# ConvFFN of a hybrid decoder trunk: three products in PSUM banks of their own, block sums made by stores that add, weight sums on VectorE

## The chip, the cores and the metric

The kernel runs on one core of a Trainium2 chip. The metric is the device time of one execution in microseconds, as the median of several runs. Profiled executions are recorded by the hardware profiler; the engines are named as in its page: PE (TensorE matmul), PEld (TensorE weight load), DVE (VectorE), ACT (ScalarE), POOL (GpSimd), SP (the queue that issues most DMAs).

## What is computed

A two-layer decoder trunk on one sequence of 1024 tokens with 1024 features, in float32. Each layer mixes tokens (layer 0: gated linear attention, layer 1: sparse attention, both with memory attention) and then runs a ConvFFN. The change touches the ConvFFN only, which runs twice:

```python
def conv_ffn(h, w_up, conv_w, conv_b, w_down):
    T = h.shape[1]
    a, b = jnp.split(h @ w_up, 2, axis=-1)
    a_pad = jnp.pad(a, ((0, 0), (CONV_WIDTH - 1, 0), (0, 0)))
    a = sum(a_pad[:, j:j + T] * conv_w[j] for j in range(CONV_WIDTH)) + conv_b
    return (jax.nn.silu(a) * b) @ w_down

# in the layer loop
x = x + conv_ffn(rmsnorm(x, g_ffn[l]), w_up[l], conv_w[l], conv_b[l], w_down[l])
```

FFN_DIM is 2816, that is 22 tiles of 128.

## The kernel before

**Number format.** Every float32 operand is split into a rounded part and a remainder, both float32r. A product of two such operands takes three matmuls: high by high, high by low, low by high (lines 1058 to 1060 in the up-projection, 1412 to 1414 in the down-projection). ACT writes the high part (line 1022, tiles `Ah` and `A`), DVE subtracts it from the source for the low part (line 1023, tiles `Al` and `A`).

**The up-projection** works on 22 units (class `Up`), one for each 128 columns of `a` and of `b`. A unit is a 2 by 2 by 2 block product (two halves of the features, `a` and `b`, two halves of the tokens) that is made with seven half-size products instead of eight, the scheme of Strassen and Winograd. `B[1]` to `B[7]` are the seven right-hand operands, made once. The left-hand operands 3, 5, 6 and 7 are sums of the unit's four raw weight blocks; method `sums` makes them in place with four additions or subtractions of 128x512 (lines 1042 to 1045), on DVE for the first four units in order and on POOL for the other 18. Each product is 4 x 3 = 12 matmuls of 128x512.

The products of a unit go into PSUM like this. Products 1 and 2 build the first half of `a` in bank `fx`; product 1 alone is kept as `s1`. Product 6 opens bank `fy`, and DVE adds `s1` to it and keeps the sum as `q` (line 1092). Product 7 goes on adding into the same bank `fy`, and DVE keeps that with `s1` as `t` (line 1097). Product 4 adds into `fy` a third time (line 1106). Products 5 and 3 share bank `fw` in the same way (lines 1102 and 1112). There are eight banks, handed out in turn.

Each half then goes through the three convolution taps (`taps`, lines 1117 to 1123, tile `fc`), SiLU (line 1138) and a multiplication by its half of `b` (lines 1107 and 1143).

**Order.** Units 0 and 1 run side by side as the opening pair. Units 2 to 5 are *early* units: their products 1 and 2 were made during the opening, while the norm was awaited, and were set aside in DRAM (`pre_d`). The list `order` alternates plain and early units (6, 2, 7, 3, 8, 4, 9, 5) and then runs the plain units 10 to 21. Method `run` writes out the order of one unit: a plain unit runs products 1, 6, 2, 7, 5, 4, 3; an early unit runs 6, then product 1 of the next unit, then 7, 5, 4, 3. `follow` adds order without a semaphore. A scheduler may then move instructions within an engine where dependences allow it. Each engine executes its own list strictly in order.

**Blocks for the down-projection.** Two units that follow each other form a pair (`mate` is the first of the pair for its second, and None for the first). The four gated halves B11, B12, B21 and B22 of a pair, or sums of them, are the right-hand operands of another seven-product scheme, the down-projection. DVE makes the four sums T1 to T4 (method `mixed`, line 1147), and SP stores seven blocks for each pair to the DRAM tile `gb_d` (line 1170). The down-projection runs 7 x 11 steps of 12 matmuls (tile `dn`); `DOWN` names the left operand and the block of each round of 11 steps, T4 in the first. A step's block is read back six steps ahead (line 1282, tile `bl`) and split by ACT and DVE three steps ahead (lines 1341 and 1342, tiles `da` and `db`).

Of the kernel before, what the change touches and what calls it, by code (L numbers as in the profile page):

```python
# [10 lines left out]
AF = mybir.ActivationFunctionType  # L11
ALU = mybir.AluOpType
# [22 lines left out]
def kernel(  # L35
# [25 lines left out]
    nc = tc.nc  # L61
# [13 lines left out]
    def U(dt=F32, s="u"):  # L75
        return wp.tile([P, HT], dt, tag="u", name=nm(s), bufs=14)
# [4 lines left out]
    def PS(s="ps"):  # L81
        return pp.tile([P, HT], F32, tag="ps", name=nm(s))
# [4 lines left out]
    def f(t):  # L87
        return t.bitcast(F32)

    def hs(half):  # L90
        return slice(half * HT, (half + 1) * HT)
# [46 lines left out]
    def follow(n, after, reason):  # L138
        tc.add_manual_dep(
            n.ins,  # L140
            after.ins.name,
            mybir.DependencyInfo(mybir.DependencyClass.NoSync, mybir.DependencyReason.DATA),
            reason=reason,
        )
# [268 lines left out]
    gb_d = dp.tile([NF // 2, 7, P, HT], F32, name="gb_d")  # L413
# [4 lines left out]
    BLK = ("B11", "T1", "B21", "B22", "T2", "T3", "T4")  # L418
# [560 lines left out]
    def ffn(l, blocks_, after):  # L979
# [25 lines left out]
        class Up:  # L1005
# [32 lines left out]

            def sums(self):
                (a0, b0), (a1, b1) = ((t[:, hs(0)], t[:, hs(1)]) for t in self.raw)  # L1040
                tt = (nc.vector if self.soon else nc.gpsimd).tensor_tensor
                tt(b1, b0, b1, ALU.add)  # L1042
                tt(b0, a0, b0, ALU.subtract)
                tt(a0, b1, a0, ALU.subtract)
                tt(a1, a1, a0, ALU.subtract)
# [40 lines left out]
                self.taps0()  # L1086

            def p6(self):
                self.Y = PS("fy")
                self.product(self.Y, 6, True, True)  # L1090
                self.q = U(s="q")
                self.opened = nc.vector.tensor_tensor(self.q, self.Y, self.s1, ALU.add)  # L1092

            def p7(self):
                self.product(self.Y, 7, False, True)
                self.t = U(s="t")
                self.drained = nc.vector.tensor_tensor(self.t, self.Y, self.s1, ALU.add)

            def p5(self):
                self.W = PS("fw")  # L1100
                self.product(self.W, 5, True, True)
                self.summed = nc.vector.tensor_tensor(self.t, self.W, self.t, ALU.add)

            def p4(self):
                self.product(self.Y, 4, False, True)
                nc.vector.tensor_tensor(self.s1, self.Y, self.s1, ALU.add)
                self.ended = nc.vector.tensor_tensor(self.c[0], self.c[0], self.s1, ALU.mult)
                self.stored = self.store("B11" if self.mate is None else "B21", self.c[0])

            def p3(self):  # L1110
                self.product(self.W, 3, False, True)
# [28 lines left out]
            def end(self):  # L1140
                self.c.append(self.taps(self.q, self.edge))
                self.act(1)
                nc.vector.tensor_tensor(self.c[1], self.c[1], self.t, ALU.mult)

            def mixed(self):
                def tt(past, *a):
                    op = nc.vector.tensor_tensor(*a)
                    if past is not None:
                        follow(op, past, "order")

                if self.mate is None:
                    t1 = U(s="t1")
                    past = yield
                    tt(past, t1, self.c[1], self.c[0], ALU.subtract)
                    self.store("T1", t1)
                    return
                self.store("B22", self.c[1])
                b11, b12 = self.mate.c
                past = yield
                tt(past, b12, self.c[1], b12, ALU.subtract)  # L1160
                self.store("T3", b12)
                past = yield
                tt(past, b11, b12, b11, ALU.add)
                self.store("T2", b11)
                past = yield
                tt(past, self.c[0], self.c[0], b11, ALU.subtract)
                self.store("T4", self.c[0])

            def store(self, what, t):
                return nc.sync.dma_start(gb_d[self.n, BLK.index(what)], t)  # L1170

        us = [Up(i, 2 <= i < PRE) for i in range(NF)]

        def each(group, *whats):
            for what in whats:
                for u in group:
                    getattr(u, what)()

        mixing = []

        def mix(past=None):
            if mixing:
                try:
                    mixing[0].send(past)
                except StopIteration:
                    mixing.pop(0)

        def ahead(then, after):
            if after is not None:
# [4 lines left out]
        def run(u, last, then, after):  # L1194
            nxt = [then] if then is not None else []
            if u.s1 is None:
                u.p1()
            u.p6()
            if after is not None:
                after.load(0)  # L1200
            if u.early:
                each(nxt, "direct")
                then.p1()
                each(last, "end")
                u.split35((then.kept, u.opened))
                ahead(then, after)
                u.p7()
                u.taps0()
            else:
                u.p2()  # L1210
                each(last[:1], "end")
                u.split35((u.kept, u.opened))
                ahead(then, after)
                u.p7()
                each(nxt, "direct")
            u.act0()
            each(nxt, "sums")
            u.p5()
            mix(u.summed)
            for v in nxt:  # L1220
                v.split67((u.acted, u.drained))
            if not u.early:
                each(last[1:], "end")
            for v in last:
                mixing.append(v.mixed())
                next(mixing[-1])
            mix(u.drained)
            u.p4()
            mix(u.ended)
            u.p3()  # L1230
            mix(u.closed)

        order = []
        for i in range(2, PRE):
# [3 lines left out]
        seq = pair + order[:-1]  # L1238
        for n, u in enumerate(seq):
            u.n, u.mate = n // 2, seq[n - 1] if n % 2 else None  # L1240
            u.soon = n < 4
        each(pair, "load", "direct")
        each(pair, "p1")
        pair[0].p2()
# [18 lines left out]
        last = pair  # L1263
        for u, then, after_ in zip(order, order[1:], order[2:] + [None]):
            run(u, last, then, after_)
            last = [u]
# [10 lines left out]
        tt = nc.vector.tensor_tensor  # L1277
# [23 lines left out]
        def operand(i):  # L1301
            p, n = steps[i]
# [35 lines left out]
                src = a21 if r == 7 else a11  # L1338
            for t, ring_, k in ((src, a_ring, 4), (raw_ring[i % AHEAD], b_ring, 3)):
                w = ring_[i % k]  # L1340
                nc.scalar.activation(w[:, hs(0)], t, AF.Copy)  # L1341
                b = tt(w[:, hs(1)], t, f(w)[:, hs(0)], ALU.subtract)  # L1342
                made = made or b
                out_.append(w)
            if prior[1] is not None:
# [72 lines left out]
        def down():  # L1418
# [3 lines left out]
            for i in range(READY):  # L1422
                operand(i)
            each(last, "end")
            for v in last:
                mixing.append(v.mixed())
                next(mixing[-1])
            while mixing:
                mix()
            back_to_exp(silu[0])  # L1430
            yield 0.0
            for i, (p, n) in enumerate(steps):
# [590 lines left out]
```

## Time and profile before

| what | value |
| --- | --- |
| device time, three runs | 2245.9, 2251.28, 2254.2 us; median 2251.28 |
| profiled execution | 2249.9 us, of which the span of the instructions is 2248.1 us |
| DVE busy in the span | 1723.6 us (77%) |
| ACT busy | 1116.3 us (50%) |
| POOL busy | 420.0 us (19%) |
| DMA moved | 285.20 MB, mean 127 GB/s |
| up-projection, first unit after the opening pair to first matmul of the down-projection | layer 0: 475.96 to 841.38 us; layer 1: 1655.56 to 2022.85 us |

A row of a timeline gives the start in us, the duration in us, engine, line, operation and tiles; in brackets the idle time before it and what ended it. Durations of neighbouring matmuls overlap, because matmuls are pipelined: one takes 0.39 us, but the next starts 0.23 us after it. A busy PE is therefore not PE at its peak, and lost time has to be read from start to start. A row of the waits gives the total in us, the number of times and the longest. PEld rows are the loads of weights into PE, which run beside the matmuls.

### The profile page before, as it was taken

How to read it: one execution, taken by the hardware profiler on the slowest of the kernel's cores; microseconds unless marked ns; L12 is line 12 of the kernel's file. 1: busy time of each engine (PE TensorE's matmuls, PEld its weight loads, DVE VectorE, ACT ScalarE, POOL GpSimd, SP SyncE). 2: the span in 40 equal slices, each digit the busy share in tenths (PEclk: the TensorE clock that was granted, in tenths of full speed). 3: DMA queues.
4: the chain of work that ended last, by engine and by line, in shares of the span. 5: the costliest groups of instructions: out<-in, count | busy, mean ns of one | idle time of the engine just before them, and what ended most of it. 6: DMA issues, size and time to landing. Idle time of an engine off the chain costs nothing.

```text
span 2248.1 us, 32203 instructions
## 1 busy us (share of the span) xinstructions
PE 2207.3 (98%) x11522; PEld 1839.3 (82%) x11522; DVE 1723.6 (77%) x3037; ACT 1116.3 (50%) x2085; POOL 420.0 (19%) x409
## 2 busy tenths in 40 slices
PE   9999999999999999999999999999999999999998
PEld 7888887777888888888888888888778888888886
DVE  6886886887877768887756778866987877768877
ACT  6564464543333335456545688874543333335445
POOL 1312210013332210000103323320013322210000
PEclk9999999999999999999999999999999999999999
DMA  6332246334332329544421111036434333329533
GB/s 228 103 104 87 79 156 215 132 127 134 129 122 99 108 78 353 169 136 141 129 85 42 48 48 36 9 116 212 138 127 132 127 122 103 106 74 349 164 94 112
DMA packets 138942, 285.20 MB, mean 127 GB/s; under 512 B 15709, under 2 KB 22446, under 8 KB 138782
## 3 DMA queue, kind: packets, MB, share of 16 engines
q1 hardware_dynamic: 130430, 263.11, 35.4%
q0 software_dynamic: 3600, 11.65, 1.5%
q10 hardware_dynamic: 4752, 8.39, 1.0%
q8 instruction: 90, 1.47, 0.3%
q14 instruction: 70, 0.57, 0.1%
HBM read 211.27 MB, written 71.83 MB: 126 GB/s over the span
## 4 chain that ended last, share of the span: by engine, by line
PE 79%; DVE 11%; ACT 4%; DMA 3%; issue 2%; SPq 0%; POOL 0%; DVEq 0%; ACTq 0%; POOLq 0%
PE dn L1413 6%; PE dn L1414 6%; PE dn L1412 6%; PE fy L1058 5%; PE fy L1060 5%; PE fy L1059 5%; PE fx L1058 3%; PE fx L1059 3%; PE fx L1060 3%; PE fw L1060 3%; PE fw L1058 3%; PE fw L1059 3%; PE op L195 2%; PE op L196 2%; PE op L194 2%
## 5 line engine op out<-in xcount | busy, mean ns | idle before, releaser
L1412 PE MATMUL dn<-db,da 128*128 128x512 f32 (+1 forms) x628 | 242.5, 386 | 0.0
L1413 PE MATMUL dn<-db,da 128*128 128x512 f32 (+1 forms) x628 | 242.1, 386 | 0.3 <-DVE db L1342 0.3
L1414 PE MATMUL dn<-db,da 128*128 128x512 f32 (+1 forms) x628 | 241.6, 385 | 0.0
L1058 PE MATMUL fy<-B,Ah 128*128 128x512 f32 x496 | 195.4, 394 | 8.5 <-DVE q L1092 7.3
L1060 PE MATMUL fy<-B,Al 128*128 128x512 f32 x496 | 194.0, 391 | 0.4 <-DVE Al L1023 0.4
L1059 PE MATMUL fy<-B,Ah 128*128 128x512 f32 x496 | 193.8, 391 | 0.0
L1042 POOL TENSOR_TENSOR wu<-wu,wu 128x512 f32<-128x512 f32 x36 | 47.2, 1311 | 730.7 <-DVE Al L1023 568.5
L1022 ACT ACTIVATE Ah<-wu 128x1024 fp32r<-128x1024 f32 x124 | 130.4, 1052 | 102.9 <-PE fy L1059 60.3
L1023 DVE TENSOR_TENSOR Al<-wu,Ah 128x1024 fp32r<-128x1024 f32 x124 | 160.8, 1298 | 8.5 <-ACT Ah L1022 7.4
L1413 PEld LDWEIGHTS dn<-db,da 128*128 128x128 f32 x628 | 117.9, 188 | 25.6 <-DVE db L1342 1.8
L1412 PEld LDWEIGHTS dn<-db,da 128*128 128x128 f32 x628 | 118.0, 188 | 24.1 <-issue 0.2
L1060 PE MATMUL fw<-B,Al 128*128 128x512 f32 x352 | 137.7, 391 | 0.0
L1059 PE MATMUL fw<-B,Ah 128*128 128x512 f32 x352 | 137.0, 389 | 0.0
L1058 PE MATMUL fw<-B,Ah 128*128 128x512 f32 x352 | 137.0, 389 | 0.0
L1414 PEld LDWEIGHTS dn<-db,da 128*128 128x128 f32 x628 | 117.9, 188 | 23.2
L1342 DVE TENSOR_TENSOR db<-bl,db 128x512 fp32r<-128x512 f32 x154 | 105.8, 687 | 27.9 <-ACT db L1341 27.3
L1058 PEld LDWEIGHTS fy<-B,Ah 128*128 128x128 f32 x496 | 93.5, 188 | 33.7 <-DVE q L1092 12.3
L1341 ACT ACTIVATE db<-bl 128x512 fp32r<-128x512 f32 x154 | 95.7, 621 | 34.0 <-PE dn L1414 26.4
L1060 PEld LDWEIGHTS fy<-B,Al 128*128 128x128 f32 x496 | 93.5, 189 | 20.9 <-DVE Al L1023 1.1
L1059 PEld LDWEIGHTS fy<-B,Ah 128*128 128x128 f32 x496 | 93.5, 188 | 19.0
L1138 ACT ACTIVATE fc<-fc 128x512 f32<-128x512 f32 x88 | 54.9, 626 | 106.3 <-DVE fc L1119 85.3
L1341 ACT ACTIVATE da<-wb 128x512 fp32r<-128x512 f32 x88 | 55.1, 629 | 99.4 <-PE dn L1413 67.4
(415 smaller groups left out, 6152.2 us busy)
## 6 DMA issues: line engine op xcount, KB each, us to landing
wu<-in_w_up_dram SPq DMA_DIRECT2D x176, 256.0 KB, 3.0
bl<-gb_d SPq DMA_DIRECT2D x154, 256.0 KB, 2.8
gb_d<-fc SPq DMA_DIRECT2D x132, 256.0 KB, 2.5
wb<-in_w_down_dram SPq DMA_DIRECT2D x44, 256.0 KB, 3.9
wa<-in_w_down_dram SPq DMA_DIRECT2D x22, 512.0 KB, 7.8
wo<-in_a_wo_dram SPq DMA_DIRECT2D x16, 512.0 KB, 3.8
xre<-om_d SPq DMA_DIRECT2D x32, 256.0 KB, 4.2
x_r<-x SPq DMA_DIRECT2D x32, 256.0 KB, 2.4
```

What stands on the lines that cost most here:

```text
L1022: a = nc.scalar.activation(hi, src, AF.Copy)
L1023: b = nc.vector.tensor_tensor(lo, src, f(hi), ALU.subtract)
L1042: tt(b1, b0, b1, ALU.add)
L1058: mm(ps, wr, hr, start=(first and j == 0), stop=False, skip_group_check=True)
L1059: mm(ps, wr, hl, start=False, stop=False, skip_group_check=True)
L1060: mm(ps, wl, hr, start=False, stop=(stop and j == 3), skip_group_check=True)
L1138: silu[0] = nc.scalar.activation(self.c[half], self.c[half], AF.Silu)
L1341: nc.scalar.activation(w[:, hs(0)], t, AF.Copy)
L1342: b = tt(w[:, hs(1)], t, f(w)[:, hs(0)], ALU.subtract)
L1412: mm(o, hi, bh, start=first, stop=False, skip_group_check=True)
L1413: mm(o, hi, bl, start=False, stop=False, skip_group_check=True)
L1414: mm(o, lo, bh, start=False, stop=stop or n == NP - 1, skip_group_check=True)
```

## The change

There are three edits in the up-projection, and one in the down-projection that follows from the second.

1. Products 6, 7 and 4 no longer share bank `fy`. Product 7 opens bank `fz`, product 4 opens bank `fv`. The running sums are made by DVE: `t` is now `fz` + `q`, the sum after product 5 goes into `s1`, and after product 4 into `t`. The number of DVE additions stays the same.
2. `mixed` and the queue of its pieces (`mix`) go. The sums T1 to T4 are made in DRAM: a gated half is stored to every block that it is the first part of, by SP, and added to every block that it is a later part of, by a DMA on POOL with `accum_op=ALU.add`. Two of the four halves of a pair are stored with the sign turned, which the gate multiplication does (`scalar_tensor_tensor` in place of `tensor_tensor`); where a block is stored negative, the down-projection turns the sign of its left operand while it splits it (rounds with left operand 2, 4 and 5). A pair has seven plain stores as before, and now also seven adding ones.
3. `sums` runs on DVE for all 22 units.

```diff
             def sums(self):
-                tt = (nc.vector if self.soon else nc.gpsimd).tensor_tensor
+                tt = nc.vector.tensor_tensor
...
             def p6(self):
-                self.Y = PS("fy")
-                self.product(self.Y, 6, True, True)
+                ps = PS("fy")
+                self.product(ps, 6, True, True)
                 self.q = U(s="q")
-                self.opened = nc.vector.tensor_tensor(self.q, self.Y, self.s1, ALU.add)
+                self.opened = nc.vector.tensor_tensor(self.q, ps, self.s1, ALU.add)
 
             def p7(self):
-                self.product(self.Y, 7, False, True)
+                ps = PS("fz")
+                self.product(ps, 7, True, True)
                 self.t = U(s="t")
-                self.drained = nc.vector.tensor_tensor(self.t, self.Y, self.s1, ALU.add)
+                self.drained = nc.vector.tensor_tensor(self.t, ps, self.q, ALU.add)
 
             def p5(self):
                 self.W = PS("fw")
                 self.product(self.W, 5, True, True)
-                self.summed = nc.vector.tensor_tensor(self.t, self.W, self.t, ALU.add)
+                self.summed = nc.vector.tensor_tensor(self.s1, self.W, self.t, ALU.add)
 
             def p4(self):
-                self.product(self.Y, 4, False, True)
-                nc.vector.tensor_tensor(self.s1, self.Y, self.s1, ALU.add)
-                self.ended = nc.vector.tensor_tensor(self.c[0], self.c[0], self.s1, ALU.mult)
-                self.stored = self.store("B11" if self.mate is None else "B21", self.c[0])
+                ps = PS("fv")
+                self.product(ps, 4, True, True)
+                nc.vector.tensor_tensor(self.t, ps, self.t, ALU.add)
+                self.ended = self.gate(0, self.t)
+                if self.mate is None:
+                    self.stored = self.store(self.c[0], "B11", "T1", "T2", "T4")
+                else:
+                    self.stored = self.store(self.c[0], "B21")
+                    self.more(self.c[0], "T4")
...
             def end(self):
                 self.c.append(self.taps(self.q, self.edge))
                 self.act(1)
-                nc.vector.tensor_tensor(self.c[1], self.c[1], self.t, ALU.mult)
-
-            def mixed(self):
...
+                self.gate(1, self.s1)
                 if self.mate is None:
...
+                    self.more(self.c[1], "T1", "T2", "T4")
+                    self.store(self.c[1], "T3")
+                else:
+                    self.store(self.c[1], "B22")
+                    self.more(self.c[1], "T2", "T3", "T4")
+
+            def gate(self, half, t):
+                c = self.c[half]
+                if (self.mate is None) == (half == 0):
+                    return nc.vector.tensor_tensor(c, c, t, ALU.mult)
+                return nc.vector.scalar_tensor_tensor(c, c, -1.0, t, ALU.mult, ALU.mult)
+
+            def block(self, what):
+                return gb_d[self.n, BLK.index(what)]
+
+            def store(self, t, *whats):
+                return [nc.sync.dma_start(self.block(w), t) for w in whats][0]
+
+            def more(self, t, *whats):
+                for w in whats:
+                    nc.gpsimd.dma_start(self.block(w), t, accum_op=ALU.add)
...
                 w = ring_[i % k]
-                nc.scalar.activation(w[:, hs(0)], t, AF.Copy)
-                b = tt(w[:, hs(1)], t, f(w)[:, hs(0)], ALU.subtract)
+                if k == 4 and r in (2, 4, 5):
+                    nc.scalar.activation(w[:, hs(0)], t, AF.Copy, scale=-1.0)
+                    b = nc.vector.scalar_tensor_tensor(
+                        w[:, hs(1)], t, -1.0, f(w)[:, hs(0)], ALU.mult, ALU.subtract
+                    )
+                else:
+                    nc.scalar.activation(w[:, hs(0)], t, AF.Copy)
+                    b = tt(w[:, hs(1)], t, f(w)[:, hs(0)], ALU.subtract)
```

How this moves instructions is seen best at the first early unit of layer 0 (unit 2). First PE, where its product 7 begins and then where its product 5 begins (`fw`, left operand `Ah_3824` and `Al_3825`). Before:

```order
L1060 MATMUL fx_4216<-B_3378,A_3532 128x512
L1058 MATMUL fy_4195<-B_3810,Ah_3822 128x512
L1059 MATMUL fy_4195<-B_3810,Ah_3822 128x512
...
L1058 MATMUL fw_4268<-B_3890,Ah_3824 128x512
L1059 MATMUL fw_4268<-B_3890,Ah_3824 128x512
L1058 MATMUL fx_4216<-B_3413,Ah_3535 128x512
L1059 MATMUL fx_4216<-B_3413,Ah_3535 128x512
L1060 MATMUL fx_4216<-B_3413,Al_3536 128x512
L1058 MATMUL fx_4216<-B_3435,Ah_3535 128x512
L1059 MATMUL fx_4216<-B_3435,Ah_3535 128x512
L1060 MATMUL fw_4268<-B_3890,Al_3825 128x512
```

The same places on PE now:

```order
L1060 MATMUL fx_4229<-B_3378,A_3532 128x512
L1058 MATMUL fz_4260<-B_3810,Ah_3822 128x512
L1059 MATMUL fz_4260<-B_3810,Ah_3822 128x512
...
L1058 MATMUL fw_4286<-B_3892,Ah_3824 128x512
L1059 MATMUL fw_4286<-B_3892,Ah_3824 128x512
L1058 MATMUL fv_4302<-B_3944,A_3531 128x512
L1059 MATMUL fv_4302<-B_3944,A_3531 128x512
L1060 MATMUL fv_4302<-B_3944,A_3531 128x512
L1058 MATMUL fv_4302<-B_3947,A_3531 128x512
L1059 MATMUL fv_4302<-B_3947,A_3531 128x512
L1060 MATMUL fw_4286<-B_3892,Al_3825 128x512
```

Product 7 keeps its place, but writes a new bank. Ahead of the first matmul that needs the low part `Al_3825`, the scheduler puts five matmuls of other work in both kernels: of the next plain unit's product 2 before, of the same unit's product 4 now. So the next plain unit runs all 12 matmuls of its product 2 between its products 6 and 7 now, and only the 7 that were left before.

Next DVE at the same unit, from the addition after product 6 on (`q`; `wu` are raw weights, `a` is a block that was set aside in DRAM). Before:

```order
L1092 TENSOR_TENSOR q_4208<-fy_4195,s_727_4110 128x512
L1119 SCALAR_TENSOR_TENSOR fc_4231<-q_4076,cs,fc_4231 128x511
L1123 SCALAR_TENSOR_TENSOR fc_4231<-edge_4092,cs,fc_4231 128x1
L1119 SCALAR_TENSOR_TENSOR fc_4231<-q_4076,cs,fc_4231 128x510
L1123 SCALAR_TENSOR_TENSOR fc_4231<-edge_4092,cs,fc_4231 128x2
L1023 TENSOR_TENSOR Al_3825<-wu_3520,Ah_3824 128x1024
L1143 TENSOR_TENSOR fc_4231<-fc_4231,t_4126 128x512
L1097 TENSOR_TENSOR t_4255<-fy_4195,s_727_4110 128x512
L1147 TENSOR_TENSOR t_742_4286<-fc_4231,fc_4094 128x512
```

The same stretch on DVE now:

```order
L1092 TENSOR_TENSOR q_4221<-fy_4208,s_731_4122 128x512
L1045 TENSOR_TENSOR wu_3522<-wu_3522,wu_3521 128x512
L1125 SCALAR_TENSOR_TENSOR fc_4244<-q_4084,cs,fc_4244 128x511
L1129 SCALAR_TENSOR_TENSOR fc_4244<-edge_4100,cs,fc_4244 128x1
L1125 SCALAR_TENSOR_TENSOR fc_4244<-q_4084,cs,fc_4244 128x510
L1129 SCALAR_TENSOR_TENSOR fc_4244<-edge_4100,cs,fc_4244 128x2
L1023 TENSOR_TENSOR Al_3825<-wu_3520,Ah_3824 128x1024
L1161 SCALAR_TENSOR_TENSOR fc_4244<-fc_4244,s_725_4069 128x512
L1098 TENSOR_TENSOR t_4273<-fz_4260,q_4221 128x512
```

One weight sum (line 1045) stands behind `q` now, and the T sum behind `t` is gone; the split that product 5 needs (line 1023) keeps its place behind the four taps of the unit before. On POOL, the 36 x 4 weight sums are gone, and 77 adding DMAs for each layer stand in their place, each behind the gate that makes its source.

More of the change, by code (lines that the diff above doesn't have):

```diff
@@ L1142, in end @@
                 self.act(1)
-                nc.vector.tensor_tensor(self.c[1], self.c[1], self.t, ALU.mult)
-            def mixed(self):
[L1146 to L1149, printed above, removed]
-                if self.mate is None:
[L1152 to L1170, printed above, removed]
+                self.gate(1, self.s1)
+                if self.mate is None:
+                    self.more(self.c[1], "T1", "T2", "T4")
[15 more added lines that the diff above has]
+                    nc.gpsimd.dma_start(self.block(w), t, accum_op=ALU.add)
         us = [Up(i, 2 <= i < PRE) for i in range(NF)]
@@ L1177, in each @@
                     getattr(u, what)()
[L1179 to L1186, printed above, removed]
         def ahead(then, after):
@@ L1218, in run @@
             u.p5()
-            mix(u.summed)
             for v in nxt:
@@ L1223, in run @@
                 each(last[1:], "end")
[L1224 to L1227, printed above, removed]
             u.p4()
-            mix(u.ended)
             u.p3()
-            mix(u.closed)
         order = []
@@ L1240, in ffn @@
             u.n, u.mate = n // 2, seq[n - 1] if n % 2 else None
-            u.soon = n < 4
         each(pair, "load", "direct")
@@ L1424, in down @@
             each(last, "end")
[L1425 to L1429, printed above, removed]
             back_to_exp(silu[0])
```

## The prediction

> **What bounds the kernel now.** I read the page first: the span, the busy shares, and the chain of work that ended last.
>
> ```profile
> span 2248.1 us, 32203 instructions
> PE 2207.3 (98%) x11522; PEld 1839.3 (82%) x11522; DVE 1723.6 (77%) x3037; ACT 1116.3 (50%) x2085; POOL 420.0 (19%) x409
> PE 79%; DVE 11%; ACT 4%; DMA 3%; issue 2%; SPq 0%; POOL 0%; DVEq 0%; ACTq 0%; POOLq 0%
> ```
>
> PE sets the time, and no edit changes the number of matmuls. So a gain can only come from PE's gaps, and work put on DVE, ACT or POOL costs only where PE then waits. How large are the gaps in the stage that the change touches? PE's timeline gives its ends (in layer 0 also the first matmul of unit 11):
>
> ```profile
> 475.96 0.39 PE L1058 MATMUL fx<-B,A 128*128 128x512 f32 x1
> ...
> 631.94 0.39 PE L1058 MATMUL fx<-B,A 128*128 128x512 f32 x1
> ...
> 841.38 0.39 PE L1412 MATMUL dn<-db,da 128*128 128x512 f32 x1
> ...
> 1655.56 0.39 PE L1058 MATMUL fx<-B,A 128*128 128x512 f32 x1
> ...
> 2022.85 0.39 PE L1412 MATMUL dn<-db,da 128*128 128x512 f32 x1
> ```
>
> From 631.94 to 841.38 run eleven plain units of 84 matmuls: 209.44 us / 924 = 0.2267 us each. That is the pitch without gaps. The whole stage has 20 units, four of them without products 1 and 2: 20 x 84 - 4 x 24 = 1584 matmuls, 359.05 us at this pitch. It takes 365.42 us in layer 0 and 367.29 us in layer 1. The excess, **6.4 + 8.2 = 14.6 us**, bounds what this stage can give. All of layer 0's lies ahead of 631.94, where early units alternate with plain ones. The waits say for what:
>
> ```profile
> PE fy L1058 <- DVE q L1092: 7.3, 6, 2.6
> PEld fy L1058 <- DVE q L1092: 12.3, 11, 3.0
> ```
>
> Eleven times product 7 wants bank `fy` before DVE has added product 6 up (`q`). The two largest cases on PE's timeline:
>
> ```profile
> 500.24 0.39 PE L1060 MATMUL fx<-B,A 128*128 128x512 f32 x1
> 502.38 0.50 PE L1058 MATMUL fy<-B,Ah 128*128 128x512 f32 x1 [1.75 <-DVE q L1092]
> ...
> 503.20 0.40 PE L1058 MATMUL fy<-B,Ah 128*128 128x512 f32 x1
> ...
> 1680.57 0.39 PE L1060 MATMUL fx<-B,A 128*128 128x512 f32 x1
> 1683.53 0.62 PE L1058 MATMUL fy<-B,Ah 128*128 128x512 f32 x1 [2.58 <-DVE q L1092]
> 1683.95 0.63 PE L1059 MATMUL fy<-B,Ah 128*128 128x512 f32 x1
> ...
> 1687.28 0.40 PE L1058 MATMUL fy<-B,Ah 128*128 128x512 f32 x1
> ```
>
> Start to start, less one pitch, they lose 502.38 - 500.24 - 0.23 = 1.91 and 2.73 us. All eleven, read so, add up to 9.4. There is a price behind the pause too. From 1683.53 to 1687.28 nine matmuls take 3.75 us instead of 2.04, which is 1.7 us more; the view of windows shows the granted clock there at 0.53:
>
> ```profile
> 1683.53:1687.07 3.54, 3.54 (x9) 2.76 (x10) 3.26 (x6) 1.88 (x3) 0.00 (x0) 0.53 0.20 74
> ```
>
> (Columns: the stretch in us; busy time and count of PE, PEld, DVE, ACT and POOL; clock; DMA share; GB/s.) Behind the other ten it is smaller: 502.38 to 503.20 is three pitches, 0.68, and took 0.82. Together 9.4 + 1.7 + 10 x 0.13 = **12.4 us**. The other 2.2 us of the excess are mostly 0.1 to 0.2 us at product 5 of the early units, which waits for its low part.
>
> Why is `q` late? DVE's and POOL's timelines just ahead of 502.38, with what DVE does later:
>
> ```profile
> 490.13 1.62 POOL L1042 TENSOR_TENSOR wu<-wu,wu 128x512 f32<-128x512 f32 x1 [143.91 <-DVE Al L1023]
> ```
> ```profile
> 491.11 1.72 DVE L1023 TENSOR_TENSOR Al<-wu,Ah 128x1024 fp32r<-128x1024 f32 x1
> 492.75 1.77 DVE L1119 SCALAR_TENSOR_TENSOR fc<-q,cs,fc 128x511 f32<-128x511 f32 x1
> ...
> 502.25 0.73 DVE L1119 SCALAR_TENSOR_TENSOR fc<-q,cs,fc 128x511 f32<-128x511 f32 x1
> ...
> 503.83 1.22 DVE L1023 TENSOR_TENSOR Al<-wu,Ah 128x1024 fp32r<-128x1024 f32 x1
> ...
> 1684.98 1.21 DVE L1023 TENSOR_TENSOR Al<-wu,Ah 128x1024 fp32r<-128x1024 f32 x1
> ```
>
> Beside POOL's weight sums the same DVE instructions take 1.72 instead of 1.22 and 1.77 instead of 0.73 us. POOL's sums hold DVE up, and `q` stands behind them in DVE's list.
>
> A sentence on the notes: the Trainium skill, "SBUF — State Buffer", section "Who interferes with whom", says that a DVE instruction with two inputs in SBUF contends with a GpSimd instruction that reads SBUF; the rows above agree (1.72 against 1.22).
>
> **Part 1, a bank each.** Product 7 opens `fz` and needs no `q`. All eleven waits go: **-12.4 us**. What is late next? Product 5's third matmul, the first to use `Al` from line 1023. Product 7 has 12 matmuls, and seven more stand ahead of that third matmul (two of `fw`, five of `fv` now). Had DVE been exactly as late as in the trace, at the first case it would be wanted at 500.47 + 19 x 0.2267 = 504.78, and `Al` ends at 503.83 + 1.22 = 505.05: 0.3 us. At the second it is wanted at 1680.80 + 4.31 = 1685.11, and `Al` ends at 1686.19: 1.1 us. So at most 1.4 us come back in these two places if DVE gains nothing; I take 0, since POOL's hold on DVE goes as well. Five banks per unit are opened instead of three; with eight in turn, one comes round after 1.6 units, some 30 us, where the addition that frees it runs within a few us of its product.
>
> **Parts 2 and 3, DVE's load.** The groups by line:
>
> ```profile
> L1147 DVE TENSOR_TENSOR fc<-fc,fc 128x512 f32<-128x512 f32 x66 | 61.8, 936 | 0.0
> L1147 DVE TENSOR_TENSOR t<-fc,fc 128x512 f32<-128x512 f32 x22 | 15.0, 683 | 0.1
> L1143 DVE TENSOR_TENSOR fc<-fc,t 128x512 f32<-128x512 f32 x44 | 30.1, 685 | 0.3 <-ACT fc L1138 0.3
> L1042 DVE TENSOR_TENSOR wu<-wu,wu 128x512 f32<-128x512 f32 x8 | 5.5, 686 | 0.0
> L566 DVE SCALAR_TENSOR_TENSOR x<-x,cs,rs 128x512 f32<-128x512 f32 x32 | 22.8, 748 | 0.1
> L491 POOL DMA_DIRECT2D om_d<-mof x16 | 8.9, 553 | 139.9 <-ACT mof L490 139.9
> ```
>
> DVE takes 36 x 4 = 144 sums at 0.686: +98.8 us. It drops the 88 T sums: -61.8 - 15.0 = -76.8. Half of the 88 gates and 66 left operands of the down-projection become the other form, at 0.748 - 0.685 = 0.063 each: +6.9. Net +29 us over two stages of 366 us, before relief: 66 T sums at 936 where 22 of the same kind take 683 show what POOL cost DVE, and the taps and splits beside POOL's sums lose more (the 1.72 and 1.77 above). Does DVE have room where it is wanted most? An early and a plain unit together, in the view of windows:
>
> ```profile
> 541.58:574.83 33.25, 33.25 (x145) 26.80 (x144) 27.31 (x38) 12.18 (x18) 12.52 (x8) 1.00 0.41 136
> ```
>
> DVE is busy 27.3 of 33.25 us with POOL's 12.5 us of sums beside it. The pair gets +8 x 0.686 - 4 x 0.87 (the mean of the 88 T sums) + 0.1 = 2.1 us, that is 29.4 without any relief and less with it, under the 32.6 us (144 x 0.2267) that PE needs. So on average it holds; what it does to single deadlines is the rival below. Cost taken: 0, between -2.2 us (the rest of the excess goes too) and +5.5 us (worked out there).
>
> **Part 2, the adding stores.** POOL loses all sums and issues 154 adding DMAs; its own DMAs take 0.553 us each (row L491), 85 us in all, 3.9 us for a pair of 33 to 38 us. Nothing else in this stage waits for POOL. SP issues seven stores for each pair as before. A block made by several DMAs is ready later, which matters only where it is read soon: at the start of the down-projection, whose first round reads T4. No row shows an add to DRAM; the nearest are plain transfers:
>
> ```profile
> om_d<-mof POOLq DMA_DIRECT2D x16, 256.0 KB, 2.4
> mem<-in_mem_dram SPq DMA_DIRECT2D x8, 256.0 KB, 7.3
> ```
>
> At that place the timelines show (layer 0):
>
> ```profile
> 851.15 0.68 DVE L1143 TENSOR_TENSOR fc<-fc,t 128x512 f32<-128x512 f32 x1
> ```
> ```profile
> 858.05 0.32 SPq L1282 DMA_DIRECT2D bl<-gb_d  x1
> ...
> 860.36 0.38 SPq L1282 DMA_DIRECT2D wa<-in_w_down_dram  x1
> ```
> ```profile
> 866.50 0.69 DVE L1310 TENSOR_TENSOR wb<-wa,wb 128x512 f32<-128x512 f32 x1 [1.80 <-DMA wa<-in_w_down_dram]
> ```
>
> The last gate ends at 851.8; three adds (T2, T3, T4) at 0.55 of issue each, and 2.4 for the last to land, give T4 at 855.9. SP issues the load of T4's last block at 858.05 now, behind the T sums, so nothing is late: cost 0. Behind that load SP holds `x` rows and the weights `wa`; DVE's line 1310 already waits for `wa` until 866.50, and step 11, which needs them, begins at 841.38 + 11 x 2.72 = 871.3. Between lie that sum, and the split by ACT and by DVE:
>
> ```profile
> L1341 ACT ACTIVATE da<-wb 128x512 fp32r<-128x512 f32 x88 | 55.1, 629 | 99.4 <-PE dn L1413 67.4
> ```
>
> 866.50 + 0.69 + 0.63 + 0.69 = 868.5, which leaves 2.8 us (an estimate: a slip of the load is taken to slip all behind it by as much). So PE waits only if the add lands after about 858.05 + 2.8 = 860.9.
>
> By the Trainium skill, "DMA: Bandwidth & Descriptors", section "Anatomy of one DMA — SWDGE (gpsimd) path", a DMA issued by GpSimd takes 2.0 us and its bytes / 436e3: my estimate from it is 2.6 us for 256 KB. The trace's 2.4 agrees for a plain store; no run here shows it for an adding one.
>
> **Sum.** The profiled execution took 2249.9 us. 2249.9 - 12.4 + 0 + 0 + 0 = 2237.5. The runs' median lies 1.4 above this execution, at 2251.3, so as a median some **2238 us** (2238.9 by the median, 2237.5 by the execution).
>
> **The rivals.**
>
> *The wait passes on to product 5.* In the order above, a weight sum (line 1045) now stands between `q` and the split that product 5 needs, and other sums stand elsewhere in DVE's list. If each of the eight early units loses one such sum in full, 8 x 0.686 = 5.5 us come back: 2238 + 5.5 = about 2243.5. For it: the split lands within some 0.1 us of its use already. Against it: before, the same four taps stood there beside POOL's sums; one held tap (1.77 - 0.73 = 1.04) costs more than the sum.
>
> *The change does not do what it says.* If `fz` or `fv` is not free when it is wanted, or product 7 is then held by its own left operand, the waits keep their size: about 2250. For it: DVE is 77% busy. Against it: the row of waits names `q` in all eleven cases, and the banks have 30 us.
>
> *Slower: the adds land late at the start of the down-projection.* An add has to read the block as well as write it, and the three may drain one after another. At 7.3 us each, the slowest transfer of this size above, T4 lands at 851.8 + 3 x 7.3 = 873.7, which is 12.8 us past 860.9. SP's list holds everything behind that load, so PE waits, once for each layer: 2238 + 25.6 = about 2264. It decides from (860.9 - 851.8) / 3 = 3.0 us per add on; with the 12.4 us gained, the kernel is slower than before from (860.9 + 6.2 - 851.8) / 3 = 5.1 us on. For it: no row shows such an add. Against it: POOL's own stores land in 2.4, and PE starts the round with ten earlier steps to run.
>
> **How the numbers follow.** Forecast 0.57, wait at product 5 0.25, no effect 0.08, late adds 0.10. 0.5% of the median is 11.3 us, about what a measurement of this kernel can tell from no change; faster by more than that is below 2240.0. The forecast, at 2238, falls on the far side of it for the most part: 0.50 of its 0.57. The wait at product 5 and no effect count as the same, but for 0.02. The late adds are slower, but for 0.01. So faster 0.52, same 0.39, slower 0.09. The range runs from 2232 to 2250. The low end is 2238 less the other 2.2 us of the excess and 4 us, the spread of the three runs around their median being 3 to 5 us; the high end takes in the wait at product 5 and no effect. Left out are the late adds (0.10) and the tails of the others, some 0.08.
>
> **What would show it.** Right: no row of waits for `q` at product 7; the stage at 359 to 361 us in both layers; sums on DVE near 0.69 and taps at 0.74 throughout; POOL at 70 to 110 us, all issues. Wrong at part 1: PE's gaps sit at `fw` line 1060 behind `Al`. Wrong at the adds: a wait of SP for POOL's DMA at 852 to 862, and gaps of `dn` near step 10. I would also be wrong if POOL's issuing held DVE as its sums did: the taps would then stay near 1.2 us and more in the trace.

## The result: slower by 0.6%

| | before | after |
| --- | --- | --- |
| device time, median | 2250.9 us (2245.9 to 2254.2, 4 runs) | 2265.0 us (2264.5 to 2270.2, 4 runs) |
| span of the profiled execution | 2248.1 us | 2262.6 us |
| ratio to before | 1 | 1.0062, 95% interval 1.0045 to 1.0079 |

The page of the profile after: span and busy shares, the chain that ended last, the costliest group of POOL, and three rows of the DMA issues (the last number is the median in us from issue to landing).

```profile
span 2262.6 us, 32372 instructions
PE 2212.7 (98%) x11522; PEld 1844.6 (82%) x11522; DVE 1713.2 (76%) x3093; ACT 1115.7 (49%) x2085; POOL 341.0 (15%) x419
...
PE 76%; DVE 12%; DMA 5%; ACT 4%; issue 3%; SPq 0%; POOL 0%; DVEq 0%; ACTq 0%; POOLq 0%
...
L1171 POOL DMA_DIRECT2D gb_d<-fc x154 | 134.0, 1130 | 913.1 <-DVE fc L1161 267.3
...
wu<-in_w_up_dram SPq DMA_DIRECT2D x176, 256.0 KB, 3.7
gb_d<-fc SPq DMA_DIRECT2D x154, 256.0 KB, 6.1
gb_d<-fc POOLq DMA_DIRECT2D x154, 256.0 KB, 6.8
```

Two of these rows in the page of before:

```profile
wu<-in_w_up_dram SPq DMA_DIRECT2D x176, 256.0 KB, 3.0
gb_d<-fc SPq DMA_DIRECT2D x132, 256.0 KB, 2.5
```

An adding DMA takes 1.13 us to issue and 6.8 us to land, the plain stores to the same blocks have gone from 2.5 to 6.1 us, and the loads of raw weights (`wu`) from 3.0 to 3.7 us. DMA's share of the chain is 5% instead of 3%. The waits of PE and ACT in the profile after (total us, times, longest) show where it is felt:

```profile
PE dn L1402 <- ACT db L1331: 10.2, 4, 5.5
PE fw L1058 <- DVE s L1103: 4.7, 7, 1.4
PE dn L1403 <- DVE db L1332: 1.8, 4, 1.0
...
ACT Ah L1022 <- DMA wu<-in_w_up_dram: 30.5, 10, 4.4
...
ACT A L1022 <- DMA wu<-in_w_up_dram: 26.0, 15, 3.2
```

Product 7's wait for `q` is gone, as forecast. In its place PE waits for two things that it hardly waited for before: the operands of the down-projection (`dn`), and the sum `s` after product 5, which frees bank `fw` for product 3 (`fw` L1058).

To see how much each stage gained or lost, I cut PE's timeline at the first matmul of each up-projection and at the first and last of each down-projection (in layer 1 at the last one ahead of the final norm's first matmuls; nine matmuls of `dn` follow them in every kernel). This cut of the up-projection includes the opening pair, which the prediction's did not. The rows after:

```profile
417.46 0.39 PE L1058 MATMUL fx<-B,A 128*128 128x512 f32 x1
...
844.80 0.39 PE L1402 MATMUL dn<-db,da 128*128 128x512 f32 x1
```

In layer 0 the up-projection takes 844.80 - 417.46 = 427.34 us. Cut so, in us:

| stage | before | after | difference |
| --- | --- | --- | --- |
| up-projection, layers 0 + 1 | 429.54 + 429.29 = 858.8 | 427.34 + 426.00 = 853.3 | -5.5 |
| down-projection, layers 0 + 1 | 212.29 + 209.88 = 422.2 | 221.55 + 217.40 = 439.0 | +16.8 |
| attention of both layers | 411.84 + 539.89 = 951.7 | 417.46 + 537.54 = 955.0 | +3.3 |

The three sum to +14.6, the difference of the two executions but for 0.1. Attention is not touched by the change; below, its first part is measured again.

**The start of the down-projection after**, where the 16.8 us are: POOL's and SP's timelines of layer 0, SP's wait between 855 and 872 us, and DVE's and PE's timelines.

```profile
857.24 2.60 POOL L1171 DMA_DIRECT2D gb_d<-fc  x3 [7.45 <-DVE fc L1160]
```
```profile
858.85 0.44 SPq L1266 DMA_DIRECT2D wb<-in_w_down_dram  x1
868.36 0.32 SPq L1266 DMA_DIRECT2D bl<-gb_d  x1
868.77 1.81 SPq L1352 DMA_DIRECT2D x<-x_r  x4
870.67 0.38 SPq L1266 DMA_DIRECT2D wa<-in_w_down_dram  x1
```
```profile
SPq L1266 <- DMA gb_d<-fc: 9.0, 1, 9.0
```
```profile
877.64 0.69 DVE L1294 TENSOR_TENSOR wb<-wa,wb 128x512 f32<-128x512 f32 x1 [6.56 <-DMA wa<-in_w_down_dram]
```
```profile
873.06 0.39 PE L1404 MATMUL dn<-db,da 128*128 128x512 f32 x1
878.92 0.79 PE L1402 MATMUL dn<-db,da 128*128 128x512 f32 x1 [5.48 <-ACT db L1331]
...
881.16 0.63 PE L1403 MATMUL dn<-db,da 128*128 128x512 f32 x1
881.59 0.63 PE L1404 MATMUL dn<-db,da 128*128 128x512 f32 x1
```

The three last adds are issued from 857.24 on. SP issues nothing between 858.85 + 0.44 and 868.36, where it loads the last T4 block, 11.1 us after the first of the three adds; before it, it waits 9.0 us for DMAs to `gb_d`, as the row of waits says. Behind it stand the loads of `wa`; DVE's line 1294 waits for them until 877.64, and step 11 on PE until 878.92, a gap of 878.92 - 873.06 - 0.23 = 5.63 us. Then PE runs slowly for a while, 0.43 us from one matmul to the next (granted clock 0.51):

```profile
878.92:883.20 4.28, 4.28 (x9) 3.06 (x10) 4.25 (x8) 2.30 (x4) 0.00 (x0) 0.51 1.03 403
```

The same happens in layer 1, with a shorter gap (3.44 us in the row):

```profile
2058.45 0.39 PE L1404 MATMUL dn<-db,da 128*128 128x512 f32 x1
2062.28 0.50 PE L1402 MATMUL dn<-db,da 128*128 128x512 f32 x1 [3.44 <-ACT db L1331]
```

Read from start to start against the pitch of 0.2267 us, PE loses 9.2 us in the first 60 us of the down-projection in layer 0 and 7.5 us in layer 1, where before loses nothing in that stretch: that is 16.7 of the 16.8 us.

### The profile page after: what moved, and what is told of

Read it like the earlier page. It is cut to its first block, busy times and chain, and to the rows that moved or that the text cites. A ratio compares the mean times of both kernels' runs of the same rounds, so it can differ in the third digit from the quotient of the medians.

```text
span 2262.6 us, 32372 instructions
## 1 busy us (share of the span) xinstructions
PE 2212.7 (98%) x11522; PEld 1844.6 (82%) x11522; DVE 1713.2 (76%) x3093; ACT 1115.7 (49%) x2085; POOL 341.0 (15%) x419
## 4 chain that ended last, share of the span: by engine, by line
PE 76%; DVE 12%; DMA 5%; ACT 4%; issue 3%; SPq 0%; POOL 0%; DVEq 0%; ACTq 0%; POOLq 0%
PE dn L1403 5%; PE dn L1402 5%; PE dn L1404 5%; PE fx L1058 3%; PE fx L1060 3%; PE fx L1059 3%; PE fw L1058 3%; PE fw L1060 3%; PE fw L1059 3%; PE op L195 2%; PE op L196 2%; PE op L194 2%; DMA wu<-in_w_up_dram 2%; PE fy L1060 2%; PE fy L1059 2%
## 5 line engine op out<-in xcount | busy, mean ns | idle before, releaser
L1171 POOL DMA_DIRECT2D gb_d<-fc x154 | 134.0, 1130 | 913.1 <-DVE fc L1161 267.3
L1023 DVE TENSOR_TENSOR Al<-wu,Ah 128x1024 fp32r<-128x1024 f32 x124 | 151.1, 1220 | 7.2 <-ACT Ah L1022 6.1
L1058 PE MATMUL fw<-B,Ah 128*128 128x512 f32 x352 | 138.0, 392 | 4.7 <-DVE s L1103 4.7
L1404 PEld LDWEIGHTS dn<-db,da 128*128 128x128 f32 x628 | 118.7, 189 | 23.6
L194 PE MATMUL op<-om,wor 128*128 128x512 f32 x256 | 101.7, 398 | 0.8 <-ACT om L230 0.8
L195 PE MATMUL op<-om,wor 128*128 128x512 f32 x256 | 100.0, 391 | 0.9 <-DVE om L231 0.9
L196 PE MATMUL op<-om,wol 128*128 128x512 f32 x256 | 99.7, 390 | 0.0
L1125 DVE SCALAR_TENSOR_TENSOR fc<-q,cs,fc 128x511 f32<-128x511 f32 x88 | 65.8, 748 | 24.4 <-ACT fc L1123 24.4
L1058 PEld LDWEIGHTS fw<-B,Ah 128*128 128x128 f32 x352 | 66.1, 188 | 21.0 <-DVE s L1103 7.7
L1058 PE MATMUL fx<-B,Ah 128*128 128x512 f32 x208 | 81.5, 396 | 1.4 <-ACT s L1082 1.4
L1022 ACT ACTIVATE A<-wu 128x512 fp32r<-128x512 f32 x44 | 27.7, 630 | 111.7 <-PE fx L1059 78.8
```

What stands on the lines that cost most here:

```text
L194: mm(ps, wr[:, k, :], hr, start=(k == 0), stop=False)
L195: mm(ps, wr[:, k, :], hl, start=False, stop=False)
L196: mm(ps, wl[:, k, :], hr, start=False, stop=(k == n - 1))
L1022: a = nc.scalar.activation(hi, src, AF.Copy)
L1023: b = nc.vector.tensor_tensor(lo, src, f(hi), ALU.subtract)
L1058: mm(ps, wr, hr, start=(first and j == 0), stop=False, skip_group_check=True)
```

## The experiments

Two theories to begin with. Theory 1: the down-projection loses because the adds land late. Theory 2: the up-projection gains only 5.5 us because PE's wait passes from product 7 to product 3. The rivals: DVE's additional load, the 40 MB of additional DMA traffic, or something outside these stages. The stages of all runs, in us, each the sum of both layers, cut as above:

| kernel | weight sums | product 7's bank | T sums | up | down | median us, ratio to before (95%) |
| --- | --- | --- | --- | --- | --- | --- |
| before | POOL | shared | DVE | 858.8 | 422.2 | 1 |
| banks_alone | POOL | own | DVE | 858.3 | 423.4 | 2249.7, 0.9997 (0.9988 to 1.0006) |
| sums_alone | DVE | shared | DVE | 847.6 | 423.5 | 2239.3, 0.9953 (0.9941 to 0.9966) |
| no_adds | DVE | own | DVE | 848.1 | 423.1 | 2239.6, 0.9954 (0.9941 to 0.9966) |
| shared_bank | DVE | shared | adds | 870.7 | 437.6 | 2277.6, 1.0124 (1.0099 to 1.0150) |
| after | DVE | own | adds | 853.3 | 439.0 | 2265.0, 1.0062 (1.0045 to 1.0079) |
| after_again | DVE | own | adds | 852.8 | 439.4 | 2261.9, 1.0055 (1.0038 to 1.0073) |
| last_pair_dve | DVE | own | adds, last pair DVE | 853.1 | 423.0 | 2244.7, 0.9982 (0.9973 to 0.9990) |
| t4_first | DVE | own | adds, T4 first | 856.9 | 432.0 | 2260.8, 1.0045 (1.0030 to 1.0060) |
| p3_bank | DVE | own, product 3 too | adds | 848.1 | 439.9 | 2256.1, 1.0033 (1.0021 to 1.0044) |
| both_mended | DVE | own, product 3 too | adds, last pair DVE | 848.1 | 421.2 | 2240.0, 0.9951 (0.9937 to 0.9966) |
| plain_pool | DVE | own | plain DMAs in their place | 847.6 | 429.7 | 2246.1, 0.9982 (0.9971 to 0.9993) |

Before's median was 2249.2 to 2250.9 us beside them.

### Without the adding stores: no_adds

Before, with edits 1 and 3 alone (`mixed` and its plain stores stay):

```diff
-                tt = (nc.vector if self.soon else nc.gpsimd).tensor_tensor
+                tt = nc.vector.tensor_tensor
...
-                self.product(self.Y, 7, False, True)
+                ps = PS("fz")
+                self.product(ps, 7, True, True)
```

> Changed: a bank each and all weight sums on VectorE stay, the adding stores go; DVE makes T1 to T4 again and SP stores them. Theory 1 (the loss sits at the start of the down-projection, where the load of T4's last block waits for the adds): both down-projections fall back to the 212.5 and 209.9 us of before, within 2 us; the up-projections stay at about 427 and 426 us; time about 2245 us, 0.25% below before. Rival (DVE's 144 weight sums or something outside these stages cost the time): the time stays above 2255 us, or the down-projections stay at 217 to 222 us.

Down-projections 213.2 and 209.9, up-projections 425.2 and 422.8, time 2239.6: theory 1 holds, and the rival that DVE's sums cost the time falls. The up-projections are 5.3 us shorter than after, which was not expected: the adds cost there too.

### Only the last pair without adds: last_pair_dve

After, where for the last pair (`self.n == NF // 2 - 1`) `end` adds on DVE and SP stores:

```diff
+                if self.n == NF // 2 - 1:
...
+                    tt(b12, self.c[1], b12, ALU.add)
+                    self.store(b12, "T3")
+                    tt(b11, b12, b11, ALU.add)
+                    self.store(b11, "T2")
+                    tt(self.c[0], self.c[0], b11, ALU.add)
+                    self.store(self.c[0], "T4")
```

> Changed as the kernel after, but the four T sums of the last pair of each layer are made by DVE and stored plainly; 70 of 77 adds for each layer stay. Theory 1: only the last adds matter, so both down-projections are within 2 us of before, SP's load of T4's last block is issued within 2 us of where before has it after the last gate (6.2 us), and the time is about 2247 us. Rival (the adds cost through their DMA traffic, 40 MB more in all, wherever they run): the time stays above 2255 us and the up-projections lose as well.

Down-projections 213.1 and 209.9: all of their loss hangs on the last seven of 77 adds of a layer. SP's timeline, from the store that follows the last gate to the last T4 load:

```profile
854.20 1.52 SPq L1184 DMA_DIRECT2D gb_d<-fc  x2
...
860.60 0.32 SPq L1283 DMA_DIRECT2D bl<-gb_d  x1
```

That is 6.4 us (before: 6.2). The up-projections stay at 853.1, so there the other 70 adds do cost something: the rival holds in part.

### One edit each: banks_alone and sums_alone

banks_alone is before with edit 1, sums_alone is before with this line:

```diff
-                tt = (nc.vector if self.soon else nc.gpsimd).tensor_tensor
+                tt = nc.vector.tensor_tensor
```

> Before with the bank each alone; weight sums on GpSimd and T sums on DVE as before. Theory 2 (product 3 waits for the drain of bank fw, since five matmuls of product 4 now stand ahead of product 5's end): no wait of product 7 for q, a new wait of fw line 1058 for the addition s of line 1103, 4 us or more in all; the two up-projections give 4 to 8 us instead of 12.4; down-projections as before; time 2243 to 2247 us. Rival (my prediction's step): no such wait, time 2238 us.

> Before with all weight sums on VectorE alone. If GpSimd's hold on DVE is what makes q late, product 7's waits for q shrink from 12.4 us to under 6 us and the time is 2243 to 2248 us. If DVE's own load makes it late, the waits stay or grow, and the time is 2251 us or more. Down-projections as before in both.

The banks alone bring nothing (858.3 against 858.8 us), and the weight sums alone bring everything (847.6), more than was expected of them. The mechanism that I expected in banks_alone, product 3, was a small part only. PE's and its weight queue's waits in banks_alone:

```profile
PE fy L1060 <- DVE Al L1023: 5.6, 7, 1.1
PE fw L1058 <- DVE s L1103: 1.9, 3, 1.3
...
PEld fy L1060 <- DVE Al L1023: 9.7, 11, 1.5
```

Product 7 waits no more, but product 6 does (`fy` is its bank alone now), at its third matmul, the first that needs the low part `Al`. DVE is as late as before, and the next thing that PE needs from it is late instead. What makes it late is seen by the same group on DVE, in banks_alone and then in sums_alone:

```profile
L1023 DVE TENSOR_TENSOR Al<-wu,Ah 128x1024 fp32r<-128x1024 f32 x124 | 168.8, 1363 | 7.5 <-ACT Ah L1022 6.3
```
```profile
L1023 DVE TENSOR_TENSOR Al<-wu,Ah 128x1024 fp32r<-128x1024 f32 x124 | 151.2, 1220 | 6.1 <-ACT Ah L1022 4.9
```

1363 ns on average in banks_alone, where 18 of a layer's 22 units have POOL's sums, and 1220 without them. At product 6's first large wait in banks_alone, this instruction takes 2.33 us beside POOL's sums (POOL's, DVE's and PE's timelines):

```profile
513.99 1.68 POOL L1042 TENSOR_TENSOR wu<-wu,wu 128x512 f32<-128x512 f32 x1 [13.43 <-DVE A L1023]
```
```profile
514.43 2.33 DVE L1023 TENSOR_TENSOR Al<-wu,Ah 128x1024 fp32r<-128x1024 f32 x1
```
```profile
516.82 0.50 PE L1060 MATMUL fy<-B,Al 128*128 128x512 f32 x1 [0.87 <-DVE Al L1023]
```

At 1.22 us it would have ended 1.1 us earlier (an estimate), which is more than the 0.87 us that PE waits. DVE takes over 144 sums, and PE itself has no row of waits for `q` left in sums_alone (its weight queue keeps 1.4 us, 12.3 before).

### The adding itself or its traffic: plain_pool

After, with the adds as plain DMAs from the same queue, so that the sums of blocks are left out:

```diff
-                    nc.gpsimd.dma_start(self.block(w), t, accum_op=ALU.add)
+                    nc.gpsimd.dma_start(self.block(w), t)
```

> The kernel after with its 154 adding DMAs as plain DMAs on the same queue (the additions of the blocks are left out: each block holds the half written last). Theory A (the adding is what is slow): GpSimd's DMAs and SP's stores to the blocks land in 2 to 3 us in the median instead of 6.8 and 6.1; the down-projections fall to within 2 us of before; time 2240 to 2246 us. Rival B (154 more DMAs of 256 KB on that queue are slow whatever they do): the landing stays near 6 us, the down-projections at 217 to 222 us and the time above 2257 us.

The rows of issue and landing in plain_pool:

```profile
L1171 POOL DMA_DIRECT2D gb_d<-fc x154 | 82.7, 542 | 954.4 <-DVE fc L1161 335.1
...
gb_d<-fc SPq DMA_DIRECT2D x154, 256.0 KB, 3.4
gb_d<-fc POOLq DMA_DIRECT2D x154, 256.0 KB, 4.2
```

Theory A for the larger part: 542 ns of issue instead of 1130, 4.2 us to landing instead of 6.8. The up-projections lose nothing now (847.6). The down-projections keep 7.5 of their 16.8 us, so the plain transfers and the waits for their landing have a price as well. That is a miss: the landing was expected at 2 to 3 us and the down-projections within 2 us of before. The time is at the upper end of what was expected.

### One after the other, or together: t4_first

```diff
-                    self.more(self.c[1], "T2", "T3", "T4")
+                    self.more(self.c[1], "T4", "T2", "T3")
```

> The kernel after, with the adds of a pair's last half issued T4, T2, T3 instead of T2, T3, T4. If the three adds drain one after another, T4's last block is readable after one add: SP issues its load some 7 us after the last gate instead of 11, the down-projections lose 3 to 4 us less each, time about 2258 us. If the three share the engines and end together, nothing changes: down-projections within 1.5 us of after.

POOL's and SP's timelines in t4_first:

```profile
855.05 2.60 POOL L1171 DMA_DIRECT2D gb_d<-fc  x3 [7.40 <-DVE fc L1160]
```
```profile
856.65 0.45 SPq L1266 DMA_DIRECT2D wb<-in_w_down_dram  x1
861.97 0.32 SPq L1266 DMA_DIRECT2D bl<-gb_d  x1
```

The load of T4 follows the first add by 6.9 us instead of 11.1, and the down-projections are 7.0 us shorter. So the three adds do not end together: the first in the queue is readable first. The time fell less than the 7 us expected: the up-projections are 3.6 us longer than in the first profile of after, with more wait at product 3; why was not tried.

### Is product 3's wait a loss of its own: p3_bank and shared_bank

p3_bank gives product 3 a bank, which costs one more DVE addition for each unit:

```diff
                 self.summed = nc.vector.tensor_tensor(self.s1, self.W, self.t, ALU.add)
+                nc.vector.tensor_tensor(self.q, self.W, self.q, ALU.add)
...
-                self.product(self.W, 3, False, True)
-                self.closed = nc.vector.tensor_tensor(self.q, self.W, self.q, ALU.add)
+                ps = PS("fu")
+                self.product(ps, 3, True, True)
+                self.closed = nc.vector.tensor_tensor(self.q, ps, self.q, ALU.add)
```

> The kernel after, with product 3 in a bank of its own as well and one more addition on DVE for each unit (44 at 0.69 us). If the wait of product 3 for the drain of bank fw is a loss by itself, it goes: the up-projections together 4 to 6 us shorter than after. If it is only where DVE's lateness shows, because the raw weights arrive late beside the adds, the wait appears at another product, and the up-projections stay within 1.5 us of after or grow.

shared_bank is after without edit 1.

> The kernel after, with products 6, 7 and 4 in one bank again; weight sums on VectorE and adding stores stay. If the separate banks bring nothing by themselves, as banks_alone measured, the up-projections stay within 2 us of after and the time within 4 us of 2265 us. If the banks hide part of the late weights that the adds cause, product 7 waits for q again, the up-projections grow by 4 us or more together, and the time is 2269 us or more.

The wait goes with the bank, and the up-projections are 5.3 us shorter, in spite of 44 more additions. So theory 2 holds for after, but the adds make that wait, and not the banks: no_adds has the banks and no such wait. Without the banks the adds cost far more: PE waits for `q` again, in shared_bank

```profile
PE fy L1058 <- DVE q L1092: 17.0, 11, 2.6
```

and the up-projections are 17.4 us longer than after. So the separate banks are worth 0.5 us beside POOL's sums, -0.5 us where no adds run, and 17.4 us where they do.

### Both mended, and after once more

> The kernel after with the last pair's sums on DVE (as last_pair_dve) and product 3 in a bank of its own (as p3_bank); 140 adding stores stay. If the two waits found are the whole price of the adds, both go together: up-projections 848 us together, down-projections 213 and 210 us, time 2238 to 2242 us, the same as no_adds (2239.6) and sums_alone (2239.3). If the adds cost anything else, it stays above 2244 us.

> The kernel after once more, unchanged, for its stages: the up- and down-projections within 2 us of its first profile. The time ahead of the first up-projection, 417.5 us there against 411.8 before and 412.1 to 415.0 in eight other runs with the same code in that part, should fall into that range again if those 5.6 us are variation between executions, and stay near 417 if the change makes them.

both_mended: 848.1 and 421.2, time 2240.0. So the two waits are the whole price of the adds, as far as these runs can tell; 140 of the 154 adds are still there. after_again repeats the stages, and reaches its first up-projection at 412.9 us, so the 5.6 us of attention in layer 0 were variation between executions. Three versions are faster than before by some 0.5%, and than after by some 1%, and can't be told apart: sums_alone, the smallest edit (one line), no_adds and both_mended.

## Why the prediction was wrong

**Where time is lost before: right.** 12.4 us of product 7's waits were there to be had: sums_alone takes 858.8 - 847.6 = 11.2 us from the up-projections. It was also right that POOL's sums made `q` late.

**Part 1, "all eleven waits go: -12.4 us": wrong.** I priced a wait at its length and gave it to the edit that removes its row. The wait was the place where DVE's lateness showed, and with the banks alone it shows at product 6, at no gain (858.3). The step "what is late next?" looked at product 5 in two places, found at most 1.4 us, and went no further round: product 6 and product 3 also wait for DVE. The gain belongs to part 3, whose own worth the sum gave as 0.

**Parts 2 and 3, DVE's load at cost 0: right as a cost.** 144 sums on DVE cost PE nothing. That they are also the whole gain was not in the sum.

**Part 2, the adds at cost 0: wrong, and the step that fails the most.** "0.55 of issue each, and 2.4 for the last to land, give T4 at 855.9" took the nearest plain transfers as the value. Measured: 1.13 to issue, 6.8 to land, and the load of T4 11.1 us after the first add of the three instead of 4.1. This costs 16.8 us in the two down-projections. Both nearest rows, 2.4 and 7.3 us, stood in the prediction; the value was taken at the favourable end, although it decides between gain and loss. The adds also cost the up-projections 5.3 us, which is not in the sum at all: beside them the raw weights arrive later. DVE's idle time ahead of the low part of a single weight block, where it waits for ACT, which waits for the load, shows it, in no_adds, after and both_mended:

```profile
L1023 DVE TENSOR_TENSOR A<-wu,A 128x512 fp32r<-128x512 f32 x44 | 30.2, 686 | 2.1 <-ACT A L1022 2.1
```
```profile
L1023 DVE TENSOR_TENSOR A<-wu,A 128x512 fp32r<-128x512 f32 x44 | 30.3, 690 | 16.2 <-ACT A L1022 16.2
```
```profile
L1023 DVE TENSOR_TENSOR A<-wu,A 128x512 fp32r<-128x512 f32 x44 | 30.3, 690 | 17.3 <-ACT A L1022 17.3
```

With all weight sums on DVE it is 2 to 7 us in the three kernels without adds, and 16 to 22 us in those with them. both_mended has it too and loses nothing: product 3's bank hides it. ACT's own total wait for `wu` would mislead here. It is 27.3 us before and 56.5 us after, but 57.3 us in banks_alone, which has no adds, and 29.3 us in shared_bank, which has them all. Here is what follows at the first plain unit that waits at product 3, by SP's, ACT's, DVE's and PE's timelines after:

```profile
516.80 0.33 SPq L1019 DMA_DIRECT2D wu<-in_w_up_dram  x1
```
```profile
521.73 0.63 ACT L1022 ACTIVATE A<-wu 128x512 fp32r<-128x512 f32 x1 [3.22 <-DMA wu<-in_w_up_dram]
```
```profile
522.39 0.69 DVE L1023 TENSOR_TENSOR A<-wu,A 128x512 fp32r<-128x512 f32 x1 [2.48 <-ACT A L1022]
...
531.29 0.68 DVE L1103 TENSOR_TENSOR s<-fw,t 128x512 f32<-128x512 f32 x1
```
```profile
532.03 0.50 PE L1058 MATMUL fw<-B,Ah 128*128 128x512 f32 x1 [0.80 <-DVE s L1103]
```

The load that ACT waits 3.22 us for was issued at 516.80 and landed 4.9 us later; the median of these loads in no_adds is 2.9 us. So here the load itself was slow. DVE stands idle 2.48 us for ACT and then works without a pause; nine us later its addition `s` is late, and PE waits for it. All seven waits at product 3 are in plain units, with all twelve matmuls of product 4 ahead of it on PE, so the five matmuls of product 4 that moved ahead in the early units, which I had suspected in banks_alone, are not the cause. Whether every late load is slow to land by itself, or whether stores that land late also hold up something behind them, wasn't told apart; plain_pool (847.6 us, loads at 3.0 us) shows that the loss goes with the adding.

**The rivals.** The slower one named the mechanism and the place: adds that drain one behind the other, SP's load of T4, `wa` behind it, step 11. Its 2264 us is close to the 2265.0 only because two misses cancel: it has 7.3 us for each add and 25.6 us for both layers, where 11.1 us for three and 16.8 us were measured, and it credits 12.4 us of gain where the up-projections gave 5.5. The slack that it goes by was about right in layer 0: the load came 868.36 - 844.80 = 23.6 us after the first matmul of `dn`, before 16.7. Less the 2.8 us of slack that is 4.1 us, and PE waited 5.6. It should have had a larger chance than 0.10: the only row of that size that was slow, 7.3 us, was on its side, and the plain rows said nothing of an add. The rival "passes on to product 5" had the right idea at the wrong product, and by the wrong cause.

**The other signs.** The sign for late adds came as named: SP waits for the adds to 868 us, and the gap of `dn` is at step 11. By the prediction's own cut the stage took 363.2 and 364.0 us where 359 to 361 was said; in sums_alone it took 360.6 and 360.5. Sums at 0.69 on DVE and taps at 0.75 came as said. POOL's issues took 134 us, where 85 was worked out; "70 to 110, all issues" also forgot POOL's work in attention, which is in the page's 341.0.

## What to carry to other kernels

A wait in a profile is where lateness shows, not what it is worth: take away the cause of the late engine (here POOL's sums beside DVE's), or look at every later product that the same engine feeds before crediting a gain. Where an operation has no row in the trace and its time decides the sign, the range and the chances must take in both ends. Work that moves off a compute engine into DMAs is not free, even where no engine seems to wait for it. Here it cost most at the last blocks, which are soon read back: keep those on the engine, as last_pair_dve does. The rest came through slower loads, and a bank of its own for the product that waited hid it.

## What was not expected of the hardware

- A 256 KB DMA from POOL that adds took 1130 ns to issue and 6.8 us to land, the same without adding 542 ns and 4.2 us. Beside the adds, SP's plain stores to the blocks landed in 6.1 us instead of 2.5, and in 3.4 us beside the plain DMAs.
- Three adds from one queue did not end together: the third was readable 11.1 us after the issue of the first began, the first after 6.9 us (after and t4_first, layer 0).
- After the 5.6 us pause PE ran at a granted clock of 0.51 for 4.3 us. Nine matmuls took 4.3 us there instead of the usual 2.0, so this pause cost about 2 us more than its length.
